# First attention of an encoder on one core: products, transposes and evictions in another order

## The chip, the cores and the metric

The kernel runs on one core of a Trainium2 chip. The metric is the device time of one execution in microseconds; three runs of the kernel before stand as its median. All times below are of that kernel.

## The reference

The input is 256 tokens of 1024 fp32 features. Two layers follow, each a half-weighted SwiGLU FFN (inner width 2816), an attention, and a second such FFN, with RMS norms before and after each. The first layer's attention is the one that the change rearranges: differential attention with 8 heads of two 64-wide parts.

```python
def _swiglu(x, wg, wu, wd):
    return (jax.nn.silu(x @ wg) * (x @ wu)) @ wd

# _diff_attention: q, k, v = split(h @ w_in); the first 16 of 64 features of q and k are rotated
sc = jnp.einsum('bqhcd,bshcd->bhcqs', qb, k) * scale
p = jax.nn.softmax(sc, axis=-1)
a = p[:, :, 0] - lam * p[:, :, 1]
o = jnp.einsum('bhqs,bshe->bqhe', a, v)
o = _rmsnorm(o, subln_g) * (1.0 - lam_init)
return o.reshape(b, s, nh * 2 * dh) @ w_out
```

The second layer's attention is a neighborhood attention; its code is not edited.

## The kernel before

Every product is done in three products of reduced precision: each weight is split into a high and a low part (`whi`, `wlo`), each activation too, and high*high, high*low and low*high are summed in one PSUM bank. Weights come from DRAM in tiles of 128x1024 fp32 (512 KB, issued on SP, four raw buffers). ScalarE makes the high part (L134) and VectorE the low part (L135), in pieces of 128x512; nine buffers hold split tiles. `W.get` requests a tile, and with it the conversions of up to four tiles beyond it and their loads (L142 to L147).

The 256 tokens are two blocks t = 0, 1 of 128. Eight PSUM banks: four "acc", two "mm", two "tr".

FFN (`ffn`): the first 512 inner columns are made by rows; from then on `gu_cols(p)` makes 256 inner columns at a time, gate and up, two halves each. `proj_col` fills an mm bank: 8 products of 512 columns (L444) and 8 of 256 (L446). ScalarE then copies the second half of the bank to SBUF (L530) and VectorE adds the first half to it (L531), which frees the bank. With two mm banks, the third column group waits until the first one's bank is free. The products with the down weights (L469) gather in the acc banks, and their weights are requested in `down`, after the evictions of the same `p`.

First attention (`attn` with key "a0"): heads come in two groups g of four, and tokens in two blocks. `v_rows`, `qk_rows` project (24 products of 512 columns each, L402), `qk_rows` also rotates; `qk_T` transposes four 128x128 blocks and splits them for scores. `scores(g, t, pr)` takes two acc banks and goes on to the softmax (L682 maxima on VectorE, L698 exponentials on ScalarE, L706 difference of the two maps). `probs_T` transposes the difference and ScalarE copies it to `aT` (L734). `av(g, t)` multiplies with the values: 16 products of 128 columns into a tr bank (L770), then four squares on ScalarE (L776), a power on GpSimd (L781) and scaling on VectorE to `o` (L787). `o_T` transposes `o` and splits it to `oT` (`split_bank`, L368 on ScalarE and L369 on VectorE). `wout(y, t, js)` multiplies the 128-wide pieces js of block t with the output weights, six products for each (L469): `y0` lies in the two mm banks, `y1` in two acc banks. `norms` (L338) makes the sum with the residual and the next normed input `xg`; `norm_T` transposes it for the next FFN.

A list planner sets the order of each engine's queue when the program is built: it plays the program through, and an engine that is free takes, of the instructions that the planner takes to be ready, the one with the lowest number. The number is the place in the code; `tc.high_priority(offset=n)` lowers it by n for what stands inside (HP = 200 for the norms, HP2 = 100 for `split_bank`, `act`, `gated`). On the chip each queue runs in that order, with semaphores for what must be waited for. (`in_turn`, L400, which also chains row products, is set only up to the first rows of the first FFN.)

Of the kernel before, what the change touches and what calls it, by code (L numbers as in the profile page):

```python
# [12 lines left out]
AF = mybir.ActivationFunctionType  # L13
ALU = mybir.AluOpType
# [11 lines left out]
HP2 = 100  # L26
# [129 lines left out]
def encoder_kernel(ctx, tc, x, norm_g, f1g, f1u, f1d, f2g, f2u, f2d,  # L156
                   dwi, dwo, dlam, dsub, nwi, nwo, rpb, ropec, maskc, out):
    nc = tc.nc
# [343 lines left out]
    def ffn(key, li, gains, xg1, xT, last, aside=None):  # L502
        accs = [[bank(ps_acc, "acc") for _ in range(2)] for _ in range(NH)]
        hT = {}

        def gu_rows(nme, t, hooks={}):
            ps = mm_tile()
            proj_rows(ps, xT, t, [(key, nme, 0, j) for j in range(KT * NC // UE)], hooks)
            return ps

        def act(g):
            s = t2p.tile([P, NC], F32, tag="t2", name=nm("s"))
            with tc.high_priority(offset=HP2):
                nc.scalar.activation(s, g, AF.Silu)  # L514
            return s

        def gated(u, s):
            a = t2p.tile([P, NC], F32, tag="t2", name=nm("a"))
            with tc.high_priority(offset=HP2):
                nc.vector.tensor_tensor(out=a, in0=u, in1=s, op=ALU.mult)  # L520
            return a

        def gu_cols(p):
            keys = [[(key, n, p * PW, j) for j in range(KT * PW // UE)] for n in "gu"]
            g = t2p.tile([P, 2, S], F32, tag="t2", name=nm("g"))
            u = t2p.tile([P, 2, S], F32, tag="t2", name=nm("u"))
            for k, y in zip(keys, (g, u)):
                for f in range(2):
                    ps = proj_col(xT, k, f)
                    nc.scalar.activation(y[:, f], ps[:, S:], AF.Copy)  # L530
                    nc.vector.tensor_tensor(out=y[:, f], in0=ps[:, :S], in1=y[:, f], op=ALU.add)  # L531
                if y is g:
                    s = act(flat(g))
            a = gated(flat(u), s)
            ht = l4p.tile([P, 2, 2, S], F32R, tag="l4", name=nm("hT"))
            split_bank(flat(ht[:, 0]), flat(ht[:, 1]), a)
            for f in range(2):
                hT[2 * p + f] = (ht[:, 0, f, :], ht[:, 1, f, :])

        def down(p, t):  # L540
            q = slice(t * P, (t + 1) * P)
            return row_steps(accs[t], lambda i: hT[2 * p + i][0][:, q], lambda i: hT[2 * p + i][1][:, q],
                             [(key, "d", 2 * p + i) for i in range(2)], p == 0, p == NPAIR - 1, t == NH - 1)

        hh = [l4p.tile([P, 4, S], F32R, tag="l4", name=nm("hT0")) for _ in range(2)]
        for f in range(4):
            hT[f] = (hh[0][:, f, :], hh[1][:, f, :])

        def to_T(a, t):
            q = slice(t * P, (t + 1) * P)  # L550
            transpose_split(a, hh[0][:, :, q], hh[1][:, :, q])

        s0 = act(gu_rows("g", 0))
        a0 = gated(gu_rows("u", 0, while_rows(xg1, xT, 1)), s0)
        s1 = act(gu_rows("g", 1))
        in_turn[0] = False
        to_T(a0, 0)
        a1 = gated(gu_rows("u", 1), s1)
        for p in range(2, NPAIR):
            gu_cols(p)  # L560
            if p == 2:
                to_T(a1, 1)
            if p == 3 and key == "f10":
                with tc.issue_after(W.last_dma.ins):
                    load_constants()
            if p == 4:
                gpre, gpost = gains()
            if p == 5 and aside is not None:
                aside()
            for d in downs_after(p):  # L570
                for t in range(NH):
                    down(d, t)
        for p in range(NPAIR - HELD, NPAIR):
            down(p, 0)
        xg = norms(0, accs[0], gpost, gpre, True)
        nxT = None if last else xt_tiles("xT")
        for p in range(NPAIR - HELD, NPAIR):
            if p == NPAIR - 1 and not last:
                norm_T(xg, nxT, 0)
            down(p, 1)  # L580
        xg = norms(1, accs[1], gpost, gpre, True)
        return xg, nxT

    def attn(key, li, gains, xg1, xT):
# [32 lines left out]
        def qk_rows(part, g, t, hooks={}):  # L617
            ps = mm_tile()
            proj_rows(ps, xT, t, keys_of(part, g), hooks)
            n = t2p.tile([P, NC], F32, tag="t2", name=nm("nat"))  # L620
            nc.scalar.activation(n, ps, AF.Copy, scale=0.125 if part == 0 else 1.0)
            nat[part, g, t] = n
            if not diff:
                return
            nb = NC // 64
            X = n.rearrange("p (b d) -> p b d", d=64)[:, :, 0:16]
            l = [list(z) for z in X.ap]
            Xs = bass.AP(tensor=X.tensor, offset=X.offset + 8, ap=[l[0], l[1], [-8, 2], [1, 8]])
            rt = t2p.tile([P, NC], F32, tag="t2", name=nm("rt"))
            r1, r2 = [rt[:, i * 16 * nb:(i + 1) * 16 * nb].rearrange("p (b d) -> p b d", d=16) for i in range(2)]  # L630
            nc.vector.tensor_tensor(out=r1, in0=X, in1=mid_bcast(rope[:, t, 0, :], nb), op=ALU.mult)
            nc.vector.tensor_tensor(
                out=r2.rearrange("p b (t e) -> p b t e", t=2), in0=Xs,
                in1=mid_bcast(rope[:, t, 1, :].rearrange("p (t e) -> p t e", t=2), nb), op=ALU.mult)
            nc.vector.tensor_tensor(out=X, in0=r1, in1=r2, op=ALU.add)
# [83 lines left out]
        def probs_T(g, qh, pr):  # L719
            ps, rz = steps.pop((g, qh, pr))  # L720
            res = []
            if not diff:
                for c, p in enumerate(ps):
                    if qh == 0:
                        aTs[g, pr, c] = [l4p.tile([P, NH, 4, P], F32R, tag="l4", name=nm("aT")) for _ in range(2)]
                    hi, lo = [v[:, qh].rearrange("p i (r q) -> p (i r) q", q=GRID_W) for v in aTs[g, pr, c]]
                    tr = transposes(flat(p)).rearrange("p i (r q) -> p (i r) q", q=GRID_W)
                    split_bank(hi, lo, flip(tr))
                return
            for c, p in enumerate(ps):  # L730
                tr = transposes(flat(p))
                a = t2p.tile([P, 4, P], F32, tag="t2", name=nm("aT"))
                if c == 0:
                    nc.scalar.activation(a, tr, AF.Copy)  # L734
                else:
                    nc.vector.tensor_copy(a, tr)
                res.append(a)
            aTs[g, qh, pr] = res, rz
# [88 lines left out]
        if diff:  # L827
            W.extra(len(W.extras))
            scores(0, 0, 0)
            scores(0, 0, 1)  # L830
            qk_rows(0, 1, 1)
            qk_T(0, 1, 0)
            scores(0, 1, 0)
            probs_T(0, 0, 0)
            scores(0, 1, 1)
            probs_T(0, 0, 1)
            o = av(0, 0)
            qk_rows(1, 1, 0)
            qk_T(0, 1, 1)
            qk_rows(1, 1, 1)  # L840
            qk_T(1, 1, 0)
            o_T(0, 0, o)
            probs_T(0, 1, 0)
            probs_T(0, 1, 1)
            o = av(0, 1)
            qk_T(1, 1, 1)
            W.extra(len(W.extras))
            gpre, gpost = gains()
            scores(1, 0, 0)
            scores(1, 0, 1)  # L850
            v_rows(1, 0)
            o_T(0, 1, o)
            scores(1, 1, 0)
            v_rows(1, 1)
            scores(1, 1, 1)
            y0 = [mm_tile() for _ in range(2)]
            wout(y0, 0, [0, 1, 2, 3])
            probs_T(1, 0, 0)
            probs_T(1, 0, 1)
            o = av(1, 0)  # L860
            y1 = [bank(ps_acc, "acc") for _ in range(2)]
            wout(y1, 1, [0, 1])
            probs_T(1, 1, 0)
            probs_T(1, 1, 1)
            o_T(1, 0, o)
            o = av(1, 1)
            wout(y0, 0, [4, 5])
            wout(y0, 0, [6, 7])
            xg = norms(0, y0, gpost, gpre, False)
            o_T(1, 1, o)  # L870
            wout(y1, 1, [2, 3])
            wout(y1, 1, [4, 5, 6])
            nxT = xt_tiles("xT")
            norm_T(xg, nxT, 0)
            wout(y1, 1, [7])
            xg = norms(1, y1, gpost, gpre, False)
            return xg, nxT
# [116 lines left out]
```

## Time and profile before

| | us |
|---|---|
| median of 3 runs | 1010.07 |
| lowest, highest | 1009.2, 1011.17 |
| profiled execution | 1012.26 |
| its span, first to last instruction | 1010.0 |
| TensorE busy in the span | 991.0 |
| VectorE, ScalarE busy | 676.2, 588.1 |

TensorE is busy 98% of the span. Busy is counted from modelled ends of overlapping products, so short idle times between products can hide in it. FFNs take most of the span; the first attention lies between about 201 and 321 us.

### The profile page before, as it was taken

What the parts mean: (1) busy time and instruction counts of PE and PEld (TensorE: products, weight loads), DVE (VectorE), ACT (ScalarE), POOL (GpSimd) and SP (SyncE); (2) the same over time, 40 slices, a digit from 0 to 9 for tenths busy, and PEclk for the clock granted to TensorE, in tenths of its full rate; (3) what the DMA queues carried; (4) which work ended last, traced back from release to release, by engine and by line L of the source; (5) the groups of instructions that cost most, each with busy time, mean ns of one, the idle gap of its engine ahead of it and who ended that gap; (6) DMA issues with size and microseconds to landing.
All of it is one profiled execution on the core that took longest, in us unless ns stands there. A gap on an engine that the chain in (4) does not pass through costs nothing.

```text
span 1010.0 us, 14628 instructions
## 1 busy us (share of the span) xinstructions
PE 991.0 (98%) x5299; PEld 839.2 (83%) x5299; DVE 676.2 (67%) x1282; ACT 588.1 (58%) x1247; POOL 20.7 (2%) x35
## 2 busy tenths in 40 slices
PE   8999999999999999999999999999999999999997
PEld 4888888888777888888888888888898888888886
DVE  6665656577777656566577576658788687556562
ACT  6655555466777555556456556546675666555551
POOL 0000000000001000000000000000000000000000
PEclk9999999999999999999999999999999999999999
DMA  7767665365533677666367677554735256666631
GB/s 259 237 199 238 186 198 185 115 206 169 197 96 108 204 218 221 204 177 204 94 203 246 194 236 225 191 149 153 240 99 172 84 167 228 190 211 186 203 110 42
DMA packets 121289, 182.83 MB, mean 181 GB/s; under 512 B 6113, under 2 KB 88161, under 8 KB 121218
## 3 DMA queue, kind: packets, MB, share of 16 engines
q1 hardware_dynamic: 121168, 181.78, 57.7%
q8 instruction: 41, 0.67, 0.3%
q14 instruction: 30, 0.25, 0.1%
q0 software_dynamic: 48, 0.13, 0.1%
q10 hardware_dynamic: 2, 0.00, 0.0%
HBM read 180.84 MB, written 1.05 MB: 180 GB/s over the span
## 4 chain that ended last, share of the span: by engine, by line
PE 84%; DMA 5%; DVE 5%; ACT 4%; issue 1%; POOL 0%; SPq 0%; DVEq 0%; POOLq 0%; ACTq 0%
PE acc L469 25%; PE mm L444 24%; PE mm L402 14%; PE mm L446 13%; DVE wlo L135 3%; DMA raw<-in_ffn_wg_dram 2%; PE mm L469 2%; PE tr L378 2%; ACT whi L134 1%; ACT p L698 1%; DMA raw<-in_na_w_in_dram 1%; PE acc L750 1%; PE tr L770 1%; DMA raw<-in_ffn_wd_dram 1%; DMA raw<-in_na_w_out_dram 1%
## 5 line engine op out<-in xcount | busy, mean ns | idle before, releaser
L135 DVE TENSOR_TENSOR wlo<-raw,whi 128x512 fp32r<-128x512 f32 x656 | 421.1, 687 | 194.0 <-ACT whi L134 104.7
L134 ACT ACTIVATE whi<-raw 128x512 fp32r<-128x512 f32 x656 | 366.8, 624 | 169.2 <-PE acc L469 45.8
L444 PE MATMUL mm<-xT,whi 128*128 128x512 f32 x1152 | 288.4, 392 | 2.0 <-DVE g L531 1.9
L444 PEld LDWEIGHTS mm<-xT,whi 128*128 128x128 f32 x1152 | 208.9, 189 | 41.8 <-DVE g L531 3.2
L469 PE MATMUL acc<-whi,hT 128*128 128x512 f32 x704 | 197.0, 391 | 0.0
L402 PE MATMUL mm<-whi,xT 128*128 128x512 f32 x544 | 177.4, 397 | 1.3 <-ACT whi L134 1.1
L446 PEld LDWEIGHTS mm<-xT,wlo 128*128 128x128 f32 x1152 | 157.1, 190 | 11.3
L446 PE MATMUL mm<-xT,wlo 128*128 128x256 f32 x1152 | 160.6, 282 | 0.0
L469 PEld LDWEIGHTS acc<-whi,hT 128*128 128x128 f32 x704 | 130.3, 188 | 25.5
L402 PEld LDWEIGHTS mm<-whi,xT 128*128 128x128 f32 x544 | 102.2, 189 | 22.4 <-ACT whi L134 1.5
L469 PE MATMUL acc<-wlo,hT 128*128 128x512 f32 x352 | 111.2, 390 | 0.0
L402 PE MATMUL mm<-wlo,xT 128*128 128x512 f32 x272 | 108.4, 398 | 0.7 <-DVE wlo L135 0.7
L469 PEld LDWEIGHTS acc<-wlo,hT 128*128 128x128 f32 x352 | 66.1, 188 | 14.1
L402 PEld LDWEIGHTS mm<-wlo,xT 128*128 128x128 f32 x272 | 51.6, 190 | 14.3 <-DVE wlo L135 4.6
L368 ACT ACTIVATE hT<-a 128x512 fp32r<-128x512 f32 x36 | 22.9, 635 | 63.9 <-DVE a L520 63.9
L531 DVE TENSOR_TENSOR u<-mm,u 128x256 f32<-128x256 f32 x72 | 30.4, 422 | 28.0 <-ACT u L530 27.7
L530 ACT ACTIVATE u<-mm 128x256 f32<-128x256 f32 x72 | 26.9, 373 | 29.6 <-PE mm L446 29.6
L530 ACT ACTIVATE g<-mm 128x256 f32<-128x256 f32 x72 | 26.7, 371 | 23.2 <-PE mm L446 23.2
L531 DVE TENSOR_TENSOR g<-mm,g 128x256 f32<-128x256 f32 x72 | 30.3, 421 | 10.2 <-ACT g L530 10.2
L343 DVE TENSOR_TENSOR yg<-acc,gain 128x512 f32<-128x512 f32 x20 | 13.7, 687 | 33.5 <-ACT junk L293 33.4
L293 ACT ACTIVATE junk<-acc 128x512 bf16<-128x512 f32 x20 | 11.8, 591 | 39.2 <-PE acc L469 39.2
L514 ACT ACTIVATE s<-g 128x512 f32<-128x512 f32 x36 | 22.8, 632 | 18.2 <-DVE g L531 18.2
(116 smaller groups left out, 802.3 us busy)
## 6 DMA issues: line engine op xcount, KB each, us to landing
raw<-in_ffn_wg_dram SPq DMA_DIRECT2D x88, 512.0 KB, 4.7
raw<-in_ffn_wu_dram SPq DMA_DIRECT2D x88, 512.0 KB, 4.5
raw<-in_ffn_wd_dram SPq DMA_DIRECT2D x88, 512.0 KB, 4.1
raw<-in_diff_w_in_dram SPq DMA_DIRECT2D x24, 512.0 KB, 4.4
raw<-in_na_w_in_dram SPq DMA_DIRECT2D x24, 512.0 KB, 4.6
gain<-in_norm_g_dram SPq DMA_DIRECT2D x11, 512.0 KB, 5.5
raw<-in_diff_w_out_dram SPq DMA_DIRECT2D x8, 512.0 KB, 4.3
raw<-in_na_w_out_dram SPq DMA_DIRECT2D x8, 512.0 KB, 4.5
```

The lines of the kernel that those rows point to most:

```text
L134: nc.scalar.activation(hi[:, e], raw[:, e], AF.Copy),
L135: nc.vector.tensor_tensor(out=lo[:, e], in0=raw[:, e], in1=hi.bitcast(F32)[:, e], op=ALU.subtract))
L343: nc.vector.tensor_tensor(out=yg[b], in0=ys[b], in1=gpost[:, HALVES[b]], op=ALU.mult)
L368: last_act[0] = nc.scalar.activation(hi, ps, AF.Copy)
L378: nc.tensor.transpose(tr[:, j * P:(j + 1) * P], src[:, j * P:(j + 1) * P], ident)
L402: m = last_pe[0] = nc.tensor.matmul(*a, **k)
L444: nc.tensor.matmul(ps, wh, xT.both(kt), start=kt == 0, stop=False)
L446: nc.tensor.matmul(ps[:, S:], wl, xT.one(0, kt), start=False, stop=kt == KT - 1)
L469: nc.tensor.matmul(ys[b], (xh, xl)[xp](i), parts[i][wp][:, 0, HALVES[b]], start=first and b not in seen, stop=last and left[b] == 0)
L514: nc.scalar.activation(s, g, AF.Silu)
L530: nc.scalar.activation(y[:, f], ps[:, S:], AF.Copy)
L531: nc.vector.tensor_tensor(out=y[:, f], in0=ps[:, :S], in1=y[:, f], op=ALU.add)
```

## The change

In `gu_cols`, the copy and the add that empty a bank go under `high_priority(offset=HP2)`. In the first attention, `qk_rows(1,1,0)` moves ahead of `av(0,0)` and `qk_T(1,1,1)` ahead of `av(0,1)`. In its last part `y0`, the output rows of the first tokens, is finished and normed ahead of `probs_T(1,1,*)` and `av(1,1)`, and the pieces of `y0` and `y1` are cut differently. Products, transposes and loads are the same in number.

```diff
                 for f in range(2):
                     ps = proj_col(xT, k, f)
-                    nc.scalar.activation(y[:, f], ps[:, S:], AF.Copy)
-                    nc.vector.tensor_tensor(out=y[:, f], in0=ps[:, :S], in1=y[:, f], op=ALU.add)
+                    with tc.high_priority(offset=HP2):
+                        nc.scalar.activation(y[:, f], ps[:, S:], AF.Copy)
+                        nc.vector.tensor_tensor(out=y[:, f], in0=ps[:, :S], in1=y[:, f], op=ALU.add)
...
             probs_T(0, 0, 1)
+            qk_rows(1, 1, 0)
             o = av(0, 0)
-            qk_rows(1, 1, 0)
             qk_T(0, 1, 1)
...
             probs_T(0, 1, 1)
+            qk_T(1, 1, 1)
             o = av(0, 1)
-            qk_T(1, 1, 1)
...
             y0 = [mm_tile() for _ in range(2)]
-            wout(y0, 0, [0, 1, 2, 3])
+            wout(y0, 0, [0, 1])
             probs_T(1, 0, 0)
             probs_T(1, 0, 1)
             o = av(1, 0)
+            wout(y0, 0, [2, 3])
             y1 = [bank(ps_acc, "acc") for _ in range(2)]
-            wout(y1, 1, [0, 1])
-            probs_T(1, 1, 0)
-            probs_T(1, 1, 1)
+            wout(y1, 1, [0])
             o_T(1, 0, o)
-            o = av(1, 1)
             wout(y0, 0, [4, 5])
             wout(y0, 0, [6, 7])
             xg = norms(0, y0, gpost, gpre, False)
+            probs_T(1, 1, 0)
+            probs_T(1, 1, 1)
+            o = av(1, 1)
+            wout(y1, 1, [1])
+            wout(y1, 1, [2, 3])
             o_T(1, 1, o)
-            wout(y1, 1, [2, 3])
-            wout(y1, 1, [4, 5, 6])
             nxT = xt_tiles("xT")
             norm_T(xg, nxT, 0)
+            wout(y1, 1, [4, 5, 6])
             wout(y1, 1, [7])
```

## Rows read from the trace of the kernel before

**Rows 1.** The page, part 1: busy time, share of the span, instructions.
```profile
PE 991.0 (98%) x5299; PEld 839.2 (83%) x5299; DVE 676.2 (67%) x1282; ACT 588.1 (58%) x1247; POOL 20.7 (2%) x35
```
**Rows 2.** The page, part 4: chain that ended last, by engine.
```profile
PE 84%; DMA 5%; DVE 5%; ACT 4%; issue 1%; POOL 0%; SPq 0%; DVEq 0%; POOLq 0%; ACTq 0%
```
**Rows 3.** Waits of TensorE's products: total us, times, longest us.
```profile
PE mm L444 <- DVE g L531: 1.9, 4, 0.9
...
PE tr L770 <- ACT aT L734: 0.9, 1, 0.9
PE tr L378 <- DVE o L787: 0.8, 1, 0.8
...
PE tr L378 <- DVE xg L318: 0.7, 1, 0.7
```
**Rows 4.** Timeline, TensorE, 252 to 262: start, length, instruction, [idle before <-releaser].
```profile
254.78 0.39 PE L402 MATMUL mm<-wlo,xT 128*128 128x512 f32 x1
256.04 1.16 PE L770 MATMUL tr<-v,aT 128*128 128x128 f32 x8 [0.87 <-ACT aT L734]
...
258.43 1.09 PE L770 MATMUL tr<-v,aT 128*128 128x128 f32 x8
...
259.82 1.99 PE L402 MATMUL mm<-whi,xT 128*128 128x512 f32 x8
```
**Rows 5.** Timeline, ScalarE, 250 to 262.
```profile
257.65 0.66 ACT L734 ACTIVATE aT<-tr 128x512 f32<-128x512 f32 x1
```
**Rows 6.** Timeline, VectorE, from 239.9.
```profile
239.42 1.89 DVE L135 TENSOR_TENSOR wlo<-raw,whi 128x512 fp32r<-128x512 f32 x3
```
**Rows 7.** Timeline, TensorE, 273 to 283.
```profile
273.55 0.60 PE L378 MATMUL tr<-ident,nat 128*128 128x128 f32 x4
...
280.79 0.27 PE L671 MATMUL acc<-qk,qk 64*128 64x256 f32 x1
281.37 0.39 PE L669 MATMUL acc<-qk,qk 64*128 64x256 f32 x2 [0.30 <-ACT p L698]
```
**Rows 8.** Timeline, VectorE, 274 to 283.
```profile
277.42 0.23 DVE L783 TENSOR_TENSOR sub<-sub,rz 128x2 f32<-128x2 f32 x2 [1.13 <-POOL sub L781]
...
278.66 2.47 DVE L682 TENSOR_REDUCE nmx<-acc 128x2 f32<-128x512 f32 x4
```
**Rows 9.** Timeline, TensorE, 302 to 319.
```profile
302.58 0.66 PE L378 MATMUL tr<-ident,p 128*128 128x128 f32 x4 [0.83 <-DVE o L787]
...
304.21 1.95 PE L770 MATMUL tr<-v,aT 128*128 128x128 f32 x16
...
311.01 0.62 PE L469 MATMUL mm<-whi,oT 128*128 128x512 f32 x2
...
318.43 0.66 PE L378 MATMUL tr<-ident,xg 128*128 128x128 f32 x4 [0.66 <-DVE xg L318]
```
**Rows 10.** Timeline, ScalarE and VectorE, 297 to 319.
```profile
297.94 0.37 ACT L293 ACTIVATE junk<-tr,rz 128x128 bf16<-128x128 f32 x1 [1.71 <-PE tr L770]
...
301.40 1.13 DVE L787 SCALAR_TENSOR_TENSOR o<-tr,sub,subg 128x128 f32<-128x128 f32 x4
...
309.72 1.12 DVE L787 SCALAR_TENSOR_TENSOR o<-tr,sub,subg 128x128 f32<-128x128 f32 x4
...
317.62 1.41 DVE L318 SCALAR_TENSOR_TENSOR xg<-h,pre,gain 128x512 f32<-128x512 f32 x2 [0.45 <-POOL pre L308]
```
**Rows 11.** Timeline, ScalarE, 530 to 541, third FFN.
```profile
535.17 1.16 ACT L134 ACTIVATE whi<-raw 128x512 fp32r<-128x512 f32 x2 [0.97 <-DMA raw<-in_ffn_wg_dram]
...
537.65 0.36 ACT L530 ACTIVATE g<-mm 128x256 f32<-128x256 f32 x1
```
**Rows 12.** Windows, second attention: us, busy us (instructions) by engine, clock, DMA.
```profile
730.00:732.00 2.00, 0.69 (x6) 0.57 (x7) 2.00 (x8) 1.57 (x3) 0.00 (x0) 1.00 0.96 307
732.00:734.00 2.00, 2.00 (x15) 1.65 (x15) 1.99 (x11) 1.30 (x4) 0.00 (x0) 0.67 0.26 92
734.00:736.00 2.00, 2.00 (x11) 2.00 (x11) 1.46 (x10) 2.00 (x9) 0.00 (x0) 0.50 0.80 244
```

## The prediction

> **What bounds the kernel now.** I read the page's busy line first: TensorE is busy 991.0 of 1010.0 us and VectorE 676 [rows 1]; then the chain that ended last, 84% of which is TensorE [rows 2]. So the work of TensorE is the floor, this change removes none of it, and what can be had are the moments in which TensorE stands. Third come its own waits [rows 3]. Four entries concern the code that the diff touches: 1.9 us in four places on the eviction of a gate bank (all four FFNs together), and in the first attention one wait each of 0.9 us (transposed probabilities), 0.8 us (output rows, `o`) and 0.7 us (`xg`). A wait of the second attention is in no edited line. Last I read the timeline of the engines around each of these waits.
>
> A wait as printed starts at the modelled end of the product before. Eight products of 512 columns take 1.99 us [rows 4], one is 0.39 long, so they start (1.99-0.39)/7 = 0.229 us apart and a successor normally starts 0.16 before its predecessor's end. I add 0.16 to each idle time.
>
> **Key rows ahead of the first values.** Before, TensorE runs 8 of the 24 products of `qk_rows(1,1,0)`, then turns to `av(0,0)` and stands 0.87+0.16 = 1.03 us, since ScalarE is still busy with exponentials and copies `aT` late [rows 4]. Nothing else was lacking: the 16 remaining key products follow later without a wait. With the key rows ahead in the code all 24 run through: the eighth starts at 254.78, the last ends at about 254.78+17*0.229 = 258.7. The second copy of `aT` ends at 257.65+0.66 = 258.31 [rows 5], so both value blocks then start at once, and the 1.03 us are gone. What is late next is that copy, by a margin of 0.4 us. What the key rows issue besides: one ScalarE copy, three VectorE rope steps, and in the weight requests 8 conversion pairs and 4 loads on SP. By the code these weights are requested four tiles ahead of use, so key weights were requested during the query rows; VectorE's last pieces before this place end at 239.42+1.89 = 241.31 [rows 6]. The conversions requested here serve the second value rows some 20 us later and cost nothing while that distance holds. `av(0,0)` ends about 1 us later than before and its `o` with it; its transposes stand behind 24 more products, which cover that. If key weights were late after all, the stall would only move. Bounds -1.1 (the wait and one change of work less) and 0. I take **-1.0**.
>
> **Key transposes ahead of the second values.** `qk_T(1,1,1)` ran behind the 16 value products, at 273.55 [rows 7]; 16 of them take (1.95-0.27)/15*16 = 1.8 us [rows 9]. Its ScalarE copy, VectorE subtract and the scores behind come up to that much sooner; it has no DMA and nothing on POOL. The wait it can shorten is the one of the scores of (1,1,0): 280.79 to 281.37, 0.30 printed, about 0.45 lost [rows 7]. They wait for exponentials, which wait for VectorE's maxima at 278.66; those stand behind the `o` steps, which began after 1.13 us of POOL [rows 8]. Sooner scores could use that VectorE gap for the maxima. Against it: the transposes take a bank and a ScalarE slot ahead of the values, and `o` of (0,1) may be late instead. Bounds -0.6 and +0.3 (the printed wait once more); I take **-0.4**, nearer to the row that shows the free VectorE.
>
> **Output rows of the first tokens end early.** The same 96 products, 16 value products per block and the same transposes stand in another order; only idle time changes.
> First idle time, on `o` of (1,0). Before: 0.83+0.16 = 1.0 us [rows 9]. From the first square at 297.94 to the end of `o` at 301.40+1.13 = 302.53 are 4.6 us; for the last block, from 306.16 (304.21+1.95) to 309.72+1.12 = 310.84, 4.7 us [rows 9, 10]. After, 12 products of `y0` and 6 of `y1` stand between values and the transposes of `o`: 18*0.229 = 4.1 us. Left: 0.55 us, a change of -0.45.
> Second, the end. Before, `y0` ends at 311.63 and the transposes of `xg` start at 318.43, 6.8 us later; the work put there is short by 0.66+0.16 = 0.8 us, while `o` of (1,1) had been hidden under the last 24 products of `y0` [rows 9, 10]. After, `av(1,1)` comes behind `y0`. Its `o` is there at the earliest 1.8+4.7 = 6.5 us after `y0`, and products [4,5,6] start after 0.45 us of transposes and a ScalarE copy like the 0.66 us of [rows 5]: 7.6 us. TensorE has until then 1.8 (values) + 18*0.229 = 4.1 (`y1` [1], [2,3]) + 0.9 (8 transposes of `xg`) + 0.45 = 7.2 us, or 5.8 if the six products of [1] were already used as filler. Idle: 0.4 to 1.8 us. The squares, POOL steps and `o` steps now share their engines with the norm of the first tokens, which the code gives the greater preference: up to 1.5 us more by the 1.4 us that its two `xg` steps alone take on VectorE [rows 10]. So 0.4 to 3.3, I take 1.4: a change of +0.6, bounds -0.4 and +2.5.
> Together **+0.2**, bounds -0.85 and +2.05. The conversions of the next FFN's gate tiles and their SP loads shift with the requests inside `wout`; they are needed only after the last product, so I cost them at nothing; without that cover a wait like the 0.97 us on a load [rows 11].
>
> **Column banks ahead of conversions.** `HP2` lowers the number by which the list planner chooses between instructions ready at the same moment. The order in each engine's queue is fixed when the program is built; the chip's lateness does not change it. So the edit only helps where the planner had an eviction and a conversion of lower number ready together. The rows say otherwise: before the eviction of the second gate bank ScalarE converts two pieces that waited 0.97 us for a load of `ffn_wg` [rows 11]. By the code these belong to the next pair of columns, requested in `down`, behind all four evictions. They were already of less preference than the eviction and went first, because the planner saw them ready sooner. What makes the bank late is a load later than planned, behind which the eviction is queued. Bounds: -1.9, all of it [rows 3], and +0.4 (one eviction of 0.36 us ahead of a conversion that is needed [rows 11]). I take **0**.
>
> **Sum.** -1.0 -0.4 +0.2 +0 = -1.2 us. The profiled execution took 1012.26 us, 2.26 outside its span of 1010.0; it would take 1011.1. It stood 2.2 above the median of 1010.07; I take the change from the median: **1008.9 us**. All bounds on one side would give -4.45 and +2.75.
>
> **Rivals.**
> *Evictions do move.* If the order on ScalarE and VectorE changes in front of the four waits, up to 1.9 us go in addition: 1007.0. For it: the wait is real and named by the profile. Against: the pieces of [rows 11].
> *The idle times only move.* Each of the three attention waits is a place where the chip is later than the planner thought; the planner again fills TensorE without a gap and the same steps (POOL, exponentials, `aT`) are late at the next place. Then 1010.1. For it: all three releasers are such chains. Against: the key rows need nothing from them.
> *Slower: the last value rows stand uncovered.* Place: between the last product of `y0` and products [4,5,6] of `y1`. If `o` of (1,1) goes through behind the whole norm, 3.3 us stand there instead of 0.8: with the first idle time -0.45 that is +2.05. In the second attention TensorE stood most of 730 to 732, and the granted clock was then 0.67 and 0.50, the lower level of 1.2 GHz, over the next 4 us, which costs 2*0.33+2*0.5 = 1.7 us [rows 12]; the same after such an idle time adds that. With the key rows' -1.0 and no gain of the scores: +2.05+1.7-1.0 = +2.75, 1012.8; without the drop 1011.1. It decides from the point where one piece of idle time is as long as the one before that drop, about 1.3 us (2.00-0.69). Against: the first attention had pieces of 0.87, 0.83 and 0.66 us [rows 4, 9], and the profile names no drop there.
> The Trainium skill ("TensorE: Matmul & The Clock Gate", section "What's actually happening") says that the throttled state is the default and that activity releases it, so a longer stand is paid for twice; the second attention agrees with its 0.50, and by that rule this rival would be 1.7 us dearer than its idle time.
>
> **How the numbers follow.** Forecast case 0.45, evictions move 0.15, idle times only move 0.22, slower 0.18. This kernel's measurement tells about 0.2% (2.0 us) from no change: below 1008.05 is faster, above 1012.1 slower. The forecast case alone spans 1007.3 to 1010.0, some four tenths of it below 1008.05; with nearly all of the second case that is 0.33 faster. Of the last case two thirds lie above 1012.1: 0.13 slower with a little of the third. Left 0.54 same. Range 1006.5 to 1011.9: it leaves out the lower part of the second case and most of the slower one with the clock drop.
>
> **What would show it.** Right: TensorE's wait on `aT` L734 is gone and the key products are 24 in a row; the wait on `o` L787 is halved; the waits on `g` L531 are again near 1.9 us, with the same conversions ahead of the evictions. A new wait on `oT` or `o` stands ahead of [4,5,6]. Wrong: a g wait near 0; or no idle time between `y0` and the end, which makes it about 1008; or a granted clock of 0.5 near the end of the first attention.

## The result, and the profile after

Five runs of the kernel after have a median of 1016.4 us (1015.48 to 1019.69), the kernel before beside them 1011.17 us; the ratio is 1.0073, 95% interval [1.0053, 1.0092]. (One run of before took 1196.89 us and is left out of the ratio, which is the estimate on record over the other runs and not the quotient of these two medians, 1.0052.) That is slower, by more than the range on record allowed.

The profiled execution of after took 1015.92 us, its span is 1013.8. I cut both spans at the first row product of each stage. The first attention grew from 119.51 us (201.13 to 320.64) to 126.25 (201.96 to 328.21), **+6.74**. All other stages together came to -3.0, nearly all of it in the second attention (126.30 to 123.44), which is not edited; more on that at the end. TensorE is as busy as before. This is the page's busy line of after, to be held against [rows 1]:

```profile
PE 991.6 (98%) x5299; PEld 842.0 (83%) x5299; DVE 676.3 (67%) x1282; ACT 587.1 (58%) x1247; POOL 20.4 (2%) x35
```

TensorE's waits in after (total, times, longest), against [rows 3]:

```profile
PE tr L378 <- DVE o L788: 4.9, 2, 4.1
PE tr L771 <- ACT aT L735: 3.0, 1, 3.0
...
PE mm L444 <- DVE g L532: 1.1, 3, 0.6
```

The wait on `aT` has not gone, it has more than tripled and, as the timeline shows, belongs to another block; the wait on `o` has grown from 0.8 to 4.9. (Below L528 all line numbers are one higher than before.) First the part that went well: TensorE's timeline from 253, against [rows 4], and from 271, against [rows 7].

```profile
253.91 0.47 PE L402 MATMUL mm<-whi,xT 128*128 128x512 f32 x1
...
257.66 1.98 PE L402 MATMUL mm<-whi,xT 128*128 128x512 f32 x8
259.48 1.95 PE L771 MATMUL tr<-v,aT 128*128 128x128 f32 x16
...
271.29 0.63 PE L378 MATMUL tr<-ident,nat 128*128 128x128 f32 x4
271.75 2.04 PE L771 MATMUL tr<-v,aT 128*128 128x128 f32 x16
```

The 24 key products stand in a row, the first values follow without a wait, and TensorE's waits of after hold none of the scores on exponentials, which were 0.30 us before [rows 7]. Then the last part, against [rows 9]:

```profile
297.96 0.76 PE L378 MATMUL tr<-ident,o 128*128 128x128 f32 x3 [0.83 <-DVE o L788]
...
305.50 0.60 PE L378 MATMUL tr<-ident,p 128*128 128x128 f32 x4
305.86 1.17 PE L469 MATMUL acc<-whi,oT 128*128 128x512 f32 x4
...
312.26 2.49 PE L771 MATMUL tr<-v,aT 128*128 128x128 f32 x16 [2.96 <-ACT aT L735]
318.81 1.16 PE L378 MATMUL tr<-ident,o 128*128 128x128 f32 x4 [4.06 <-DVE o L788]
```

The transposes of the last probabilities are over at 306.1, but the values that need their copies start at 312.26. In between TensorE spends the 14 products that were meant to cover `o` (305.86 to 309.31), then stands 3.0 us, and after the values 4.1 us more. ScalarE shows why the copies are late (against [rows 10]):

```profile
299.11 0.60 ACT L368 ACTIVATE oT<-tr 128x512 fp32r<-128x512 f32 x1 [0.79 <-PE tr L378]
304.40 0.60 ACT L293 ACTIVATE junk<-mm 128x512 bf16<-128x512 f32 x1 [4.69 <-PE mm L469]
...
309.55 2.17 ACT L134 ACTIVATE whi<-raw 128x512 fp32r<-128x512 f32 x4
311.63 1.06 ACT L735 ACTIVATE aT<-tr 128x512 f32<-128x512 f32 x2
314.85 0.37 ACT L293 ACTIVATE junk<-tr,rz 128x128 bf16<-128x128 f32 x1 [2.16 <-PE tr L771]
```

Both copies stand behind the whole norm of the first tokens and six conversions, although the first one's transposes ended at 299.5 and ScalarE was idle for 4.69 us once it had made `oT` (299.71 to 304.40). What holds them is the order in which the queue was written. Last the windows (us, busy us of PE, PEld, DVE, ACT, POOL, granted clock, DMA):

```profile
308.00:312.00 4.00, 1.31 (x6) 0.75 (x4) 3.81 (x8) 3.80 (x9) 0.56 (x1) 1.00 0.20 39
312.00:316.00 4.00, 2.49 (x16) 2.20 (x16) 2.02 (x4) 1.77 (x7) 0.00 (x0) 0.71 0.71 228
316.00:320.00 4.00, 1.19 (x6) 1.05 (x7) 1.49 (x7) 0.75 (x4) 1.02 (x1) 0.50 0.38 126
320.00:324.00 4.00, 4.00 (x14) 3.18 (x13) 1.38 (x2) 1.57 (x3) 0.00 (x0) 0.51 0.02 4
```

After the first stand the granted clock falls to the lower of its two levels, 1.2 GHz (0.71, 0.50 and 0.51 from 312 to 324), and TensorE, at work again from 318.81, runs about five more microseconds at it.

### The profile page after: what moved, and what is told of

Its sections match the earlier page's. It is cut to its first block, busy times and chain, and to the rows that moved or that the text cites. A ratio compares the mean times of both kernels' runs of the same rounds, so it can differ in the third digit from the quotient of the medians.

```text
span 1013.8 us, 14626 instructions
## 1 busy us (share of the span) xinstructions
PE 991.6 (98%) x5299; PEld 842.0 (83%) x5299; DVE 676.3 (67%) x1282; ACT 587.1 (58%) x1247; POOL 20.4 (2%) x35
## 3 DMA queue, kind: packets, MB, share of 16 engines
HBM read 180.84 MB, written 1.05 MB: 179 GB/s over the span
## 4 chain that ended last, share of the span: by engine, by line
PE 89%; ACT 4%; DVE 4%; DMA 2%; issue 1%; POOL 0%; DVEq 0%; POOLq 0%; ACTq 0%
PE acc L469 26%; PE mm L444 25%; PE mm L402 17%; PE mm L446 13%; PE tr L378 3%; DVE wlo L135 2%; PE mm L469 2%; ACT whi L134 1%; DMA raw<-in_ffn_wg_dram 1%; ACT p L699 1%; PE acc L751 1%; PE tr L771 1%; PE mm L429 1%; PE mm L430 1%; PE mm L428 1%
```

## The experiments

Eleven kernels, each timed beside the kernel before. "First attention" is read from the profiled execution as above (before 119.51, after 126.25), one profile for each kernel; the ratio is to before. The two FFNs between the attentions, in which only the column banks' edit differs, took 370.2 to 371.9 us in the profiles (e8 left out, whose attention holds part of them), so a few tenths between two stages tell nothing.

| | first attention, us | ratio, 95% interval |
|---|---|---|
| e1 both key moves alone | 116.72 | 0.9965 [0.9949, 0.9981] |
| e2 last part alone | 130.59 | 1.0091 [1.0069, 1.0114] |
| e3 after, aT in buffers of its own | 123.76 | 1.0050 [1.0031, 1.0069] |
| e4 after, spare products in the gaps | 124.51 | 1.0041 [1.0027, 1.0056] |
| e5 e3 and a scratch tile of its own | 122.62 | 1.0035 [1.0020, 1.0051] |
| e6 after, norm behind the last values | 124.77 | 1.0052 [1.0033, 1.0072] |
| e7 as after, but values ahead of y0's end | 117.11 | 0.9973 [0.9956, 0.9990] |
| e8 e5, xg transposed ahead of o | see below | 1.0003 [0.9989, 1.0017] |
| e9 key rows alone | 118.21 | 0.9990 [0.9968, 1.0012] |
| e10 key transposes alone | 117.92 | 0.9986 [0.9964, 1.0009] |
| e11 e6, norm not preferred | 122.23 | 1.0020 [1.0006, 1.0033] |

**Which part costs: e1 and e2.** Edits: of the diff only its second and third hunk (e1), only its last (e2).

> The kernel before with only the key rows ahead of the first values and the key transposes ahead of the second values; the last part and the column banks are as before. Theory (the two moves remove the idle time that the trace of after has lost between 240 and 290 us): 6.1 us lost there become about 3.3, and nothing behind it moves, so 2 to 3 us less than before, ratio 0.997 to 0.998. Rival (the idle times only move to the last part): ratio 0.999 to 1.001. Second rival (part of the loss of after comes from these moves): ratio above 1.002.

> The kernel before with only the new order of the last part (output rows of the first tokens ahead of the second tokens' values). Theory (the whole loss sits in this part): the idle time between 290 and 330 us goes from 3.0 to about 12 us, with the same waits on aT (3 us) and on o of (1,1) (4 us), so 8 to 10 us more than before, ratio 1.008 to 1.010. Rival (it needs the key moves as well, because they shift the weight requests): less than 4 us more, ratio below 1.004.

The theories held, e2 with more than I gave it: -2.79 us for the key moves, +11.08 for the last part alone (+9.53 on top of the key moves, 126.25-116.72). The rival that the idle times only move falls with e1. The losses of the last part are the same two waits in e2, 2.93 on aT and 4.05 on o; 1.2 of the 1.55 us between 11.08 and 9.53 lie in the values `av(1,1)`, which ran 3.68 us in e2, with the clock already low from 313.3, and 2.49 in after.

**Which piece of the last part: e7.** After, with three lines moved up:

```diff
             wout(y1, 1, [0])
+            probs_T(1, 1, 0)
+            probs_T(1, 1, 1)
             o_T(1, 0, o)
+            o = av(1, 1)
             wout(y0, 0, [4, 5])
             wout(y0, 0, [6, 7])
             xg = norms(0, y0, gpost, gpre, False)
-            probs_T(1, 1, 0)
-            probs_T(1, 1, 1)
-            o = av(1, 1)
```

> e1 (key rows and key transposes moved) with the pieces of y0 and y1 cut as in after, but the values of the second tokens ahead of the last pieces of y0, as before. Theory (the loss comes from the norm's place alone, not from the cut): as e1 within 1.5 us, ratio 0.995 to 0.998; o of (1,1) is hidden under the last 12 products of y0 and the 18 of y1. Rival (the cut, which leaves fewer products behind the first values, carries part of the loss): 2 us or more above e1, ratio 0.999 or above.

It takes 117.11 us, 9.1 less than after and 0.4 more than e1. So the whole loss comes from the place of these three lines; how the pieces are cut costs nothing that shows. TensorE's timeline of e7 in the last part:

```profile
297.39 0.66 PE L378 MATMUL tr<-ident,p 128*128 128x128 f32 x4 [0.83 <-DVE o L788]
...
309.46 0.60 PE L378 MATMUL tr<-ident,o 128*128 128x128 f32 x4
311.32 0.73 PE L469 MATMUL acc<-whi,oT 128*128 128x512 f32 x2 [1.27 <-ACT oT L368]
```

`o` of (1,1) is not waited for at all; the 0.83 us are `o` of (1,0), as in before and after. A wait of 1.27 us on `oT` stands in place of the one on `xg`.

**Why the copies are late: e3.** My first reading was that conversions and norm have preference on ScalarE. The program itself speaks against it: built with copies and value steps of the last block 400 ahead in preference, all five queues come out as in after. A second candidate is the pool: yg, xg, aT and o take their buffers from one pool. With eleven buffers in place of ten the queues of TensorE, VectorE and ScalarE again come out unchanged, so it isn't scarcity. (Neither was run, the orders being those of after.) Left was that the buffers of one pool are dealt in the order of the code:

```diff
-                a = t2p.tile([P, 4, P], F32, tag="t2", name=nm("aT"))
+                if (g, qh) == (1, 1):
+                    if pr == 0:
+                        two = l4p.tile([P, 2, 4, P], F32, tag="l4", name=nm("aT"))
+                        late.extend([two[:, 0], two[:, 1]])
+                    a = late[pr]
+                else:
+                    a = t2p.tile([P, 4, P], F32, tag="t2", name=nm("aT"))
```

> The kernel after, with the transposed probabilities of the last block in the two halves of one buffer of the 4 KB pool instead of two buffers of the 2 KB pool from which the norm takes yg and xg. Theory (the planner deals the buffers of one pool in the order of the code, so the aT copies were planned behind the last buffer of the norm, xg, though their transposes were done): the first copy stands directly behind oT, the values start 4 to 5 us sooner, TensorE's wait on aT (3.0 us) is gone, the wait on o of (1,1) falls from 4.1 to 1 us or less since the products of y1 are then left as filler, and no half clock follows: 7 to 9 us less than after, 1007.5 to 1009.5. Rival (ScalarE is simply full with the norm and the conversions): the copies stay late by 2 us or more, total within 2 us of after.

Half right. ScalarE in e3:

```profile
297.50 0.60 ACT L368 ACTIVATE oT<-tr 128x512 fp32r<-128x512 f32 x1 [0.79 <-PE tr L378]
297.99 0.59 ACT L741 ACTIVATE aT<-tr 128x512 f32<-128x512 f32 x1
...
308.83 0.35 ACT L293 ACTIVATE junk<-tr,rz 128x128 bf16<-128x128 f32 x1
```

And TensorE:

```profile
304.33 2.21 PE L777 MATMUL tr<-v,aT 128*128 128x128 f32 x16
...
315.31 1.16 PE L378 MATMUL tr<-ident,o 128*128 128x128 f32 x4 [5.56 <-DVE o L794]
```

The first copy stands directly behind `oT`, as forecast, and the wait on aT is gone: the values run from 304.33 to 306.54. So it was the shared pool that held the copies. That its buffers are dealt in code order is the reading that fits: e6 below leaves the pool shared and only puts the norm's call behind in the code, and there too the first copy stands directly behind `oT`. But the first of their squares comes 2.3 us after that, and `o` is ready at 315.94, 9.4 us behind the values where after and before take 4.7. TensorE's wait on `o` is 5.6 us, not 1, the clock falls here too (0.50 from 312.3 to 319.2), and the total is 2.5 us less in the stage, not 7 to 9.

**Why the squares are late: e5.** The same kind of hidden order, in another place: all squares write a result that nobody reads to one tile, `junk`.

```diff
+    junk2 = const.tile([P, P], BF16, name="junk2")
...
-                square(ob[:, hd * P:(hd + 1) * P], rzs[hd // 2][:, 0, hd % 2:hd % 2 + 1], ss[:, hd:hd + 1])
+                square(ob[:, hd * P:(hd + 1) * P], rzs[hd // 2][:, 0, hd % 2:hd % 2 + 1], ss[:, hd:hd + 1],
+                       junk2 if (g, qh) == (1, 1) else None)
```

> e3 with one thing more: the four squares of the last values write their unused result to a scratch tile of their own, not to the one that the squares of the norm write too. Theory (two writes of one tile are kept in the order of the code, so in e3 the squares of the values had to stand behind the last square of the norm, though the values were done 2.3 us sooner): two squares go ahead of the second square on h, the squares end 1.5 to 2 us sooner, o with them, and TensorE's wait on o falls from 5.6 to 2.5 to 4 us: 2 to 3 us less than e3, ratio to before 1.001 to 1.003. Rival (ScalarE and VectorE are simply full there with norm and conversions): o at the same place within 0.5 us, ratio 1.004 to 1.006.

```profile
307.18 0.35 ACT L294 ACTIVATE junk<-tr,rz 128x128 bf16<-128x128 f32 x1
...
309.86 0.36 ACT L294 ACTIVATE junk<-tr,rz 128x128 bf16<-128x128 f32 x1
```

The first square starts 1.65 us sooner than in e3, the wait on `o` falls to 4.2 us, just above what I expected, and 1.1 us go in the stage, not 2 to 3. So the scratch tile did order the squares, but it was the smaller part. The rest goes the way of its rival, full engines: between values and `o` there are two squares of the norm and two conversions on ScalarE, then on VectorE the two steps of xg and three conversions, and the chain takes 8.0 us.

**The norm by its place: e6 and e11.** In e6 the call of `norms` moves behind `av(1, 1)`; e11 also takes its preference away (`offset=0` for this call).

> The kernel after with one call moved in the code: the norm of the first tokens stands behind the values of the second tokens, not ahead of them; buffers and scratch tile as in after, and y0 is still finished first. Theory (only the place of the norm in the code, by pool buffers and scratch tile, held copies and squares back): aT copies directly behind their transposes, no wait on aT, squares directly behind the values, o about 6 us after the values; TensorE's wait on o 1 to 2.5 us, and up to 2 us new on xg, since the norm is now later: 4 to 7 us less than after, ratio 0.999 to 1.003. Rival (finishing y0 first costs by itself, since only 18 products are left as filler for a chain of 4.7 us): no more than 2 us less than after, ratio 1.005 or above.

> e6 (norm of the first tokens behind the values in the code) with that one norm at the ordinary preference instead of 200 ahead. Theory (in e6 the norm's steps cut in between the four steps of o on VectorE and cost 2.3 us there): the four steps of o stand together, TensorE's wait on o is one of 1.8 to 2.2 us instead of 1.8, 0.5 and 2.1, and 2 to 3 us of the first attention's 124.8 us go, unless xg is then late: its transposes have moved behind 18 of the 24 last products and have cover. Ratio 1.001 to 1.004. Rival (the wait only moves to xg): first attention within 0.7 us of e6.

In e6 the waits on aT went, as forecast; the first copy follows `oT` of 300.14:

```profile
300.63 0.60 ACT L735 ACTIVATE aT<-tr 128x512 f32<-128x512 f32 x1
```

But the time did not go: 1.5 us less than after instead of 4 to 7, and a ratio of 1.0052, which are the figures of its rival. VectorE shows the four steps of `o` broken up by the preferred norm, and TensorE waits 1.84, 0.46 and 2.08 us for them:

```profile
313.52 0.35 DVE L788 SCALAR_TENSOR_TENSOR o<-tr,sub,subg 128x128 f32<-128x128 f32 x1
313.79 0.68 DVE L343 TENSOR_TENSOR yg<-mm,gain 128x512 f32<-128x512 f32 x1
...
315.46 1.41 DVE L354 SCALAR_TENSOR_TENSOR h<-yg,post,h 128x512 f32<-128x512 f32 x2
316.79 0.61 DVE L788 SCALAR_TENSOR_TENSOR o<-tr,sub,subg 128x128 f32<-128x128 f32 x2
```

In e11 they stand together (312.57, 1.12 long) and 2.5 us go, as expected. One wait of 1.85 us on `o` stays, and one of 0.69 on `oT`. It is 5.1 us above e7 all the same: with `y0` finished first, `o` has only the last 14 products as cover, and the clock falls behind the wait, so that two products take 1.05 us there and 0.62 at the full clock. No run splits the 5.1 us between the two. The window of e11:

```profile
316.00:320.00 4.00, 4.00 (x11) 3.13 (x10) 3.55 (x8) 1.45 (x4) 0.94 (x1) 0.50 0.18 21
```

**Ready work behind the wait: e8.** In e5 the transposes of xg, ready at 310.5, stand in TensorE's queue behind those of `o`. The edit swaps the two in the code.

> e5 with the transposes of xg of the first tokens ahead of those of o of (1,1) in the code. By its queue TensorE then has the transposes of xg and 13 row products of the next FFN to do while it waits for o. Theory (the rest of the loss is TensorE standing in front of o with work ready behind it in its queue): the wait on o shrinks to below 1 us, a new one of 1 to 2 us stands in front of the first products of xg, 1.5 to 3 us less than e5, ratio 0.998 to 1.001. Rival (the row products of the FFN come before their weights are split, or the copies of xT before o's, so that the wait only changes its name): ratio within 0.001 of e5.

The ratio falls from 1.0035 to 1.0003, inside the range that I gave. Row products of the FFN now lie inside this stage, so I compare from the start of the attention to the FFN's first column product: before 142.8, e5 145.8, e8 142.6 us (e1 140.0), 3.2 us less than e5 where I had given up to 3. TensorE waits 0.26 us for xg, 0.75 for the first copy to xT and 1.16 for a bank before the second xg; `o` is no longer waited for in this place:

```profile
315.82 0.60 PE L379 MATMUL tr<-ident,o 128*128 128x128 f32 x4
```

**The clock by itself: e4.** 27 extra products on a constant tile, their result unused, lie in the two gaps of after.

```diff
-            o = av(1, 1)
             wout(y1, 1, [1])
             wout(y1, 1, [2, 3])
+            fb = bank(ps_acc, "acc")
+            spare(11)
+            o = av(1, 1)
+            spare(16)
```

In the code `av(1,1)` now stands behind [1] and [2, 3]; TensorE's queue of after has it there already.

> The kernel after, with 11 extra products of 512 columns on a constant tile while TensorE waits for aT, and 16 while it waits for o of (1,1); their result is used by nothing, all other products keep their order. It prices the clock by itself. Theory (the half clock that follows the two waits costs about 2 us on top of them): granted clock 1.0 between 313 and 324 us, waits otherwise at the same places, 1.5 to 2.5 us less than after, ratio to before 1.003 to 1.005. Rival (the slower clock costs nothing since TensorE is waiting anyway): within 0.7 us of after, ratio 1.006 to 1.007.

```profile
312.00:316.00 4.00, 3.68 (x25) 2.48 (x24) 3.02 (x5) 2.25 (x7) 0.00 (x0) 1.00 0.70 179
316.00:320.00 4.00, 3.18 (x15) 1.40 (x13) 1.49 (x7) 1.27 (x6) 1.02 (x1) 1.00 0.62 213
320.00:324.00 4.00, 3.75 (x21) 2.98 (x21) 1.93 (x3) 1.69 (x3) 0.00 (x0) 1.00 0.01 4
```

The clock stays at 1.00, the copies and `o` come no sooner (values at 110.66 us of the stage, after 110.30), and the stage takes 1.74 us less. That is the price of the lower clock on top of the waits, as forecast; the ratio points the same way (1.0041 against 1.0073, with intervals that just overlap).

**The two key moves apart: e9 and e10.**

> The kernel before with only the key rows ahead of the first values. Theory (the prediction's first term was right): the wait of 0.87 us on aT is gone and the 24 key products run through; the first attention takes 1.0 to 1.3 us less than the 119.5 us of before, and the lost time between 280 and 290 us stays near 2.0. Rival (the gain of e1 lies in both moves together): the wait on aT is gone but comes back at the next values or scores, first attention within 0.5 us of before.

> The kernel before with only the key transposes ahead of the second values. Theory (the second term, -0.4, was too small: besides the printed wait of 0.30 us the scores of (1,1,0) lost 0.28 and 0.52 us and several changes of work of 0.15 us): the wait of the scores on p is gone, the first attention takes 1.3 to 1.7 us less than before, the wait on aT at 256 us stays at 0.9. Rival (the size of the prediction, -0.4, was right and the rest of e1 came from the key rows): 0.2 to 0.6 us less.

-1.30 and -1.59 us in the stage, together 2.89 against 2.79 for e1: they add up. In e10 the wait of the scores on p is gone, as forecast. In e9 the lost time of the scores stayed as it was; it lies at 277 to 279 there, not at 280 to 290 as I had written. The ratios of the two are not told from 1 at this number of runs; the stages are what separates them.

## Why the prediction was wrong

**What failed is the term "output rows of the first tokens end early"**: +0.2, bounds -0.85 and +2.05; measured +9.5. By its pieces:

- *First idle time, on `o` of (1,0), 1.0 to 0.55.* It stayed at 0.83 printed, as in [rows 9]. I had 18 products between values and transposes; TensorE did 14 (293.67 to 297.13), since the planner had used four products of `y0` [2, 3] ahead of the values while they waited for aT.
- *The values `av(1,1)` directly behind `y0`.* This was taken for granted, and it is the mis-step. I let the transposes of p and their copies follow `y0` without asking what the copies are queued behind. Both came at 311.63, 5.5 us after the later one's transposes, 3.0 us of it as a new wait of TensorE. The fillers that I had counted for `o` were spent in that time. e3 shows that the order came from sharing the pool, not from a full ScalarE.
- *The chain of `o` shares its engines with the norm: up to 1.5 us more.* In after it cost nothing: the copies were so late that the norm was over, and the chain took its 4.7 us (314.75 to 319.44). Where values were in time (e3, e5), the chain took 4.7 and 3.3 us more (in e3 with the order by the scratch tile in it), about three and two times my bound.
- *Second idle time, 1.4 us, bounds 0.4 to 3.3.* 4.1 us, as nothing was left to fill it; the transposes of xg, which I had counted as filler, stand behind those of `o` in the queue. e8 shows what that was worth.
- *The clock*, which the term did not hold: at least 1.74 us (e4).

Sum: 3.1 (aT) + 4.2 (o) - 0.8 (the old wait on xg) + 1.7 (clock) = 8.2 of the 9.5 us. The remaining 1.3 is in no single row; no run separates it, and its cause stays open.

The prediction's own sign of being wrong, a granted clock of 0.5 near the end of the first attention, came.

**The slower rival** named the right place, between the last product of `y0` and [4, 5, 6] of `y1`, and the right extra price for the clock (1.7 us). That the prices agree is partly luck: its 1.7 came from about 3.3 us at the lower clock [rows 12], and in after the clock is low for about 10, of which TensorE waits 4.1. Its wait was too small for the same reason as mine: it also began with values in time. Its mark for the drop, a piece of 1.3 us, is no limit: in e7 TensorE stands 1.27+0.16 us at 310 and the clock stays at 1.00. The Trainium skill's rule, quoted there, that the throttled state is the default ("TensorE: Matmul & The Clock Gate", section "What's actually happening") agrees with the 0.50 of the windows of after and the 1.00 of e4.

**Key rows, -1.0, bound -1.1:** right in the mechanism, a little small; -1.30 in e9, of which 1.03 is the wait. **Key transposes, -0.4, bound -0.6:** too small; -1.59 in e10. I took the printed wait alone. Between 269 and 289 before, TensorE changes often from one shape of product to another, and the starts at such a change lie 0.06 to 0.28 us further apart than within one shape (0.229 us for 512 columns, 0.118 for a pair of scores, 0.113 for values, 0.109 for transposes). The scores stood there in broken pieces between row products; with the key transposes ahead they stand in two blocks. What the starts are further apart comes to 3.0 us in 23 places before and to 1.8 in 17 places of the same work in e10. Of the 1.2 us between them 0.46 lie in front of the scores that waited for exponentials; 0.4 of the 1.59 us stand in no row that I found.

**Column banks, 0:** right. Built with this edit alone, all five queues have the order of before. The waits on g that the profile shows vary by themselves: e2, e1, e9 and e10 have the evictions of before, and 0.5, 1.6, 1.7 and 0.5 us of it. So the 1.1 of after is no gain, and "near 1.9" was a poor test of this step.

The **forecast from the median**, and not from the profiled execution, was right to do so: the profile of before had 2.9 us in its second attention that after's did not have, so the profiled runs differ by only 3.7 us, while the ratio of 1.0073 is worth 7.

## What to carry to other kernels

When a step moves ahead of another in the code, look for what the two share beside engines: buffers of one pool and scratch tiles bind the later one to the earlier, whatever its preference. Count a filler only if nothing that is ready earlier in the queue can use it up first. The version to keep is e1, the key moves without the last part: 0.9965 [0.9949, 0.9981] of before; e7, with the pieces cut anew, is level with it.

## What the runs showed of the hardware

**One order, several lengths.** The second attention, the same code in all these kernels, took 126.30 us in the profile of before, 127.51 in e1, 123.44 in after and 124.66 in e4; over the thirteen profiles 123.4 to 128.7. In before and e1 TensorE waits 1.4 and 2.6 us there for a split of qk, and the granted clock then falls to 0.5 (in e1 0.51 over 728 to 734); in e5, the longest, it waits 2.7. In after the wait is 0.9 and the clock 1.00 throughout 716 to 740. So up to 5 us of a profile's difference can come from there, and stages must be compared one by one.

**GpSimd beside VectorE.** The power on GpSimd (L781 of before) takes 1.01 to 1.04 us in before and after, and 1.39 for the last values in e3, e5 and e8. These are its row in e3, and the one of VectorE there:

```profile
312.65 1.39 POOL L788 TENSOR_TENSOR sub<-sub,mhalf 128x4 f32<-128x4 f32 x1 [3.41 <-DVE sub L785]
312.48 0.68 DVE L135 TENSOR_TENSOR wlo<-raw,whi 128x512 fp32r<-128x512 f32 x1
```

A conversion on VectorE, with both inputs in SBUF, runs from 312.48 to 313.16, 0.51 us into the power; in e5 one from 311.11 to 311.80 lies 0.52 us over the power that starts at 311.28. Spans on GpSimd are rough, but the smaller power of the norms (L308), which runs beside many different steps, separates this. In before:

```profile
316.65 0.94 POOL L308 TENSOR_TENSOR pre<-pre,mhalf 128x1 f32<-128x1 f32 x1 [3.40 <-DVE pre L305]
316.48 0.69 DVE L135 TENSOR_TENSOR wlo<-raw,whi 128x512 fp32r<-128x512 f32 x1
```

And in e7, where VectorE's step has one input in PSUM:

```profile
311.46 0.56 POOL L308 TENSOR_TENSOR pre<-pre,mhalf 128x1 f32<-128x1 f32 x1 [3.40 <-DVE pre L305]
311.30 0.69 DVE L369 TENSOR_TENSOR oT<-tr,oT 128x512 fp32r<-128x512 f32 x1
```

Over the thirteen profiles it takes 0.55 to 0.56 us alone (55 places) or beside a step of VectorE with an input in PSUM (157), and 0.86 to 0.94 in all 71 places where a conversion was already running: 0.31 more where that ran 0.46 us into the power, 0.38 more where it ran 0.52. In 16 places the conversion started 0.11 to 0.28 us after the power, and neither was longer. The Trainium skill ("SBUF — State Buffer", section "SBUF: two separate sides") says that GpSimd and VectorE share a pair of ports that a VectorE step with two SBUF inputs, if it starts first, holds for its whole length while a GpSimd step that reads SBUF waits; the 0.31 and 0.38 us agree with that.
